# A delta-net stage in a new fixed order: values after the inversion, weights one item ahead, raw loads in GpSimd's queue

## The chip, the cores and the metric

The kernel runs on one core of a Trainium2 chip. The metric is the device time of one execution in microseconds, taken as the median of several runs. A profiled execution gives a trace of the same program; times "at" something are microseconds from the start of its span.

## The reference

Two layers, each a mixer and a convolutional feed-forward block, both with a residual and a layer norm. Layer 0's mixer is the gated delta net, to which the whole change belongs; layer 1's is a retention. Everything is fp32, sequence 1024, width 1024. The delta net, cut to what matters:

```python
proj = h @ w_in                                   # q, k, v: 8 heads x 128 each; z; a, b
qkv = silu(causal_dwconv(qkv, conv_w))            # 4 taps
q, k = l2norm(q) * dk**-0.5, l2norm(k);  beta = sigmoid(b)
gc = cumsum(-exp(a_log) * softplus(a + dt_bias))  # in each chunk
kk = where(strict, (k * beta) @ k.T * decay, 0)   # decay = exp(gc_i - gc_j), causal
u, w = solve(kk + eye, [v * beta, k * beta * exp(gc)])
qk = where(causal, q @ k.T * decay, 0)
def step(state, ...):                             # over chunks
    v_new = u - w @ state
    o = (q * exp(g)) @ state + qk @ v_new
    state = state * exp(g_last) + (k * exp(g_last - g)).T @ v_new
o = rmsnorm(o) * norm_w * silu(z)
return o @ w_out
```

The kernel takes chunks of 128 instead of the reference's 64, which is the same sum in another grouping.

## The kernel before

**Stages.** A matrix product is done as three float32r products (`mm3`): each operand is split into a high and a low part (`split`: ScalarE copies the high part, VectorE subtracts it). Up to some 78 us the kernel computes the conditioning vector, the modulated input `hT` in two halves of 512 positions, and the first projections. From there to about 620 us runs the delta net proper. Then comes `gate_phase` (output times the silu of z) and `layer_tail` (output projection, norm, feed-forward), and layer 1.

**The delta net's order.** It is written as Python generators, one for each stream of work, and `run` (L725) merges them: it keeps a clock `clk` of TensorE time, in which every matmul has a cost, and always resumes the runnable stream with the lowest priority number. A stream yields a number (wake me so many us later on that clock; these are the latencies in `LAT`), a tuple from `after_ev` (wake me once these events are emitted) or a condition (`take`: wait for buffers of a kind). Each matmul of that part goes through `pq` (L705), which chains it to the one before: TensorE's order is therefore fixed when the program is built, whatever then happens on the chip. The other engines' orders are set by the framework's own scheduler.

The streams that matter here, for heads in pairs p = 0..3 and quads g = 0, 1:

- `t_decay(p)` (L831): the decay matrices U of the pair's heads, in `aux` tiles (four exist; the recurrence of a head gives one back). It waits for the gates, for the pair before it (event `DD`, p - 1) and, in the second quad, for the first quad's inversion.
- `t_path(g)` (L843): for each head of the quad two groups of eight key products k kT, `LAT["kk"]` = 3.6 us apart, normalized into U (L872); then the inversion of 32x32 blocks by a loop of small VectorE operations (L889 to L894), two transposes and a ScalarE copy (L898 to L902). Event `T`.
- `t_chain(p)` (L913): copies the inverted blocks into tiles R and T0 on ScalarE, VectorE and GpSimd (L928, L930, L950), emits `T0`, waits `LAT["T0"]` = 8 us and then assembles the 128x128 inverses by small matmuls (32x32, then 64x64).
- `prep(p)` (L1006): transposes the pair's value features on TensorE into `acc` banks, and VectorE multiplies them out of there (L1014); then the same for decayed keys.
- `scan(p, h)` (L1050): the recurrence over eight chunks. `tail(p, h, q4)` (L1104): per half, the norm of the output (its power on GpSimd, L1111), transpose, and the store of `oTd` to DRAM from ScalarE's queue (L1118).
- `filler(items)` (L1150): all remaining projections, with the lowest priority: TensorE does them when no other stream can run. An item `("c", t)` is a projection with convolution, `"s"` the same with the result parked in DRAM (`qd`), a later `"c"` of a parked key loads it back, `"z"` is a gate projection (stored as `zd`), `"h"` finishes one begun before. Each has 48 matmuls of 128x128 by 128x512. Its weights are fetched by `load_w` (L100) when the item begins. After each item `bg_step` runs a unit of background work, among it loads of `ada_w` tiles (`mvw`, L227), which share the two buffers of the weights' tag `wr`.

PSUM has eight banks in this kernel: four `acc`, two `mm`, two `sc`.

**The gate phase** (L1224): for each head a tile `zg` of the stored gates is loaded, the output is loaded back as `raw` (two loads of 256 KB, L1242), and VectorE multiplies the two (L1243). Both loads are issued in SP's queue, which issues in order. Each raw load also sets `anchor["x", 0]`: the loads of x rows and of an `ada_b` row for the output projection are put behind the last of them in SP's queue (`after(key)`, L214 and L292).

Of the kernel before, what the change touches and what calls it, by code (L numbers as in the profile page):

```python
# [16 lines left out]
D = 1024  # L17
# [4 lines left out]
GH = 8  # L22
# [11 lines left out]
def trunk_kernel(ctx: ExitStack, tc, A):  # L34
    nc = tc.nc
    pe, act, dve, pool, sp = nc.tensor, nc.scalar, nc.vector, nc.gpsimd, nc.sync
# [45 lines left out]
    def hs(half):  # L82
        return slice(half * HALF, (half + 1) * HALF)

    xs = [dr.tile([S, D], F32, tag=f"xs{i}", name=f"xs{i}") for i in range(3)]
    oTd = [dr.tile([GH, P, S], F32, tag="oTd0", name="oTd0")]
# [5 lines left out]
    anchor = {}  # L92
# [4 lines left out]
    def kn(ap):  # L97
        return ap.rearrange("p (k n) -> p k n", n=P)

    def load_w(src, tags=("wh", "wl"), raw="wr", eng=dve):  # L100
        wr = tl(raw, [P, D])
        anchor["w"] = sp.dma_start(wr, src)
        wh = tl(tags[0], [P, D], F32R, name="wh")
        wl = tl(tags[1], [P, D], F32R, name="wl")
        split(wh, wl, wr, eng)
        return kn(wh), kn(wl)
# [73 lines left out]
    for k in range(KT):  # L180
        w = tl("hTa", [P, D], name="mvw")
# [313 lines left out]
    ssq = {}  # L495
# [223 lines left out]
    def after_ev(*names):  # L719
        return ("ev", names)  # L720
# [108 lines left out]
            give(home, 2)  # L829

    def t_decay(p):  # L831
        yield after_ev(("g",), ("DD", p - 1), ("T", p // 2 - 1))
        for h in pairs[p]:
            yield from take("aux", 1)
            U[h] = tl("aux", [P, NCH, P], name="U")
            yield from decay(h)
        yield LAT["mm"]
        for h in pairs[p]:
            act.activation(flat(U[h]), flat(U[h]), AF.Exp)
            sp.dma_start(Ld[h], flat(U[h]))  # L840
        emit(("DD", p), LAT["exp"])

# [162 lines left out]

    def prep(p):  # L1006
        heads = pairs[p]
        yield after_ev(("T", p // 2), *[("f", 2 * GH + h) for h in heads])
        for q4 in range(2):
            for h in heads:  # L1010
                pt = acc_tile()
                for c in range(4):
                    ptr(pt[:, c * P:(c + 1) * P], fx(2 * GH + h, q4 * 4 + c))
                dve.tensor_tensor(v4(feats[2 * GH + h][q4]), v4(pt), bc(ir[h][:, q4s(q4)], P), ALU.mult)  # L1014
                yield LAT["mm"]
        emit(("v", p))
        yield after_ev(("Ufree", p))
        for h in heads:
            for q4 in range(2):
                pt = acc_tile()  # L1020
                for c in range(4):
                    ptr(pt[:, c * P:(c + 1) * P], fx(GH + h, q4 * 4 + c))
                dve.tensor_tensor(U[h][:, q4s(q4)], v4(pt), bc(edl[:, q4s(q4), h], P), ALU.mult)
                yield LAT["mm"]
        emit(("kd", p))
# [122 lines left out]
            emit(("f", h), LAT["ld"])  # L1148

    def filler(items):  # L1150
        for kind, ti in items:
            if kind == "c" and ti in away:
                yield from take("qkv", 2)
                feats[ti] = two("qkv", F32, "qkv")
# [4 lines left out]
            if kind == "h":  # L1159
# [9 lines left out]
                else:  # L1169
                    emit(("f", first[ti]), LAT["fv"])  # L1170
                continue
            w = load_w(A["gdn_wz" if kind == "z" else "gdn_wqkv"][ti])
            prev = None
            if kind != "z":
                feats[ti] = []
# [20 lines left out]
            if kind != "z":  # L1196
# [5 lines left out]
                    emit(("f", ti), LAT["fv"])  # L1202
            bg_step(acc_tile)

    LAT = {"kk": 3.6, "exp": 3.2, "ld": 6.0, "g1": 12.0, "gm": 3.0, "mm": 2.2, "T": 6.0, "X": 3.4, "fs": 4.85, "T0": 8.0, "t1": 2.0, "t2": 3.3, "t3": 1.7, "D": 2.7, "s1": 1.9, "s2": 1.4, "s3": 1.8, "tail": 12.5, "ssq": 9.3, "fv": 4.0}
    events["T", -1] = events["DD", -1] = 0.0
    pairs = [(2 * p, 2 * p + 1) for p in range(GH // 2)]
    c, z = "c", "z"
    K, V = GH, 2 * GH
    s = "s"  # L1210
    quads = [tuple(range(4)), tuple(range(4, 8))]
    items = [("h", 1), ("h", 2), ("h", 3), (c, K + 2), (c, K + 3), (z, 0), (c, V), (c, V + 1), (c, V + 2), (c, V + 3), (c, 1),
             (s, 2), (s, 3), (s, K + 4), (s, K + 5), (z, 1), (z, 2), (z, 3), (c, K + 4), (c, K + 5), (c, K + 6),
             (c, K + 7), (s, 6), (s, 7), (c, V + 4), (c, V + 5), (c, V + 6), (c, V + 7), (c, 4), (c, 5),
             (z, 4), (z, 5), (z, 6), (z, 7)]
    todo = [(-1.0, gates()), (9.0, filler(items)), (0.3, t_path(0)), (2.3, t_path(1)), (0.9, load_q(1)), (2.9, load_q(3))]
    for p in range(4):
# [6 lines left out]
    def gate_phase(units, mixer, n, tags, early=(), held={}):  # L1224
        raws = []
        for k in range(n):
            gs = []
            if k in early:
                g = tl("aux", [P, S], name="zg")
                sp.dma_start(g, zd[k])  # L1230
                gs = [g[:, hs(hf)] for hf in range(2)]
                bg_step()
            else:
                accs = gemm_feat(units[k], hT)
                for hf in range(2):
                    cv = tl("cv", [P, 516], name="sg")[:, 0:HALF]
                    act.activation(cv, accs[hf], AF.Silu)
                    gs.append(cv)
            raw = held.get(k) or two(tags[k], F32, "raw")
            for hf in range(2):  # L1240
                if k not in held:
                    anchor["x", mixer] = sp.dma_start(raw[hf], oTd[mixer][k][:, hs(hf)])  # L1242
                dve.tensor_tensor(raw[hf], raw[hf], gs[hf], ALU.mult)  # L1243
            raws.append(raw)
        return raws
# [507 lines left out]
    g1 = two("auh", F32, "g1")  # L1753
# [81 lines left out]
    for t in range(4):  # L1835
        x = tl("cv", [P, 516], name="xlo")[:, 0:HALF]
# [271 lines left out]
```

## Time and profile before

| | us |
|---|---|
| median of 3 runs | 2917.15 |
| the runs | 2920.1, 2917.15, 2911.29 |
| profiled execution | 2919.49 |
| its span | 2917.7 |
| delta net, gate phase and start of the output projection | 78 to 660 |

| DMA issues touched by the change | count, KB each | us to landing (median) |
|---|---|---|
| `wr<-in_gdn_wqkv`, SP | 24, 512 | 3.5 |
| `wr<-in_gdn_wz`, SP | 8, 512 | 3.6 |
| `mvw<-in_ada_w`, SP (whole kernel) | 80, 512 | 4.5 |
| `raw<-oTd`, SP | 16, 256 | 3.5 |
| `zg<-zd`, SP | 8, 512 | 5.4 |

How to read the rows further down: PE is TensorE's matmuls, PEld its weight loads, DVE VectorE, ACT ScalarE, POOL GpSimd, SP the engine that issues most DMAs; "SPq" and "POOLq" are DMA issues in these engines' queues. A row gives engine, line, operation, `out<-in`, shapes and how many were merged. Matmuls are pipelined, so the length of one (0.4 us) is more than its pitch; the pitch is read from long rows of them.

### The profile page before, as it was taken

To read this page: it belongs to the slowest core of one execution; us is meant where nothing else is said; L and a number is where in the kernel's file an instruction comes from. 1 tells how busy PE (TensorE), PEld (TensorE's weight loads), DVE (VectorE), ACT (ScalarE), POOL (GpSimd) and SP (SyncE) were. 2 spreads that over 40 slices of the span, in tenths; PEclk is the share of its full clock that TensorE was granted. 3 is DMA by queue.
4 is the path that set the end of the run, shared out by engine and by line. 5 is a ranking of instruction groups with operands and counts; after the bars stand their busy time and mean duration, and the time that the engine had idled before them with its cause. 6 is when DMAs were issued, how large, how long until landed. Compare 5 with 4: busy or idle time off the path is not lost.

```text
span 2917.7 us, 38768 instructions
## 1 busy us (share of the span) xinstructions
PE 2799.6 (96%) x13594; PEld 2288.3 (78%) x13594; DVE 2183.0 (75%) x3874; ACT 1299.3 (45%) x2387; POOL 494.8 (17%) x509
## 2 busy tenths in 40 slices
PE   8999999999999999998999999999999999999997
PEld 6787887877788788887877877777777788888886
DVE  6796678576789888768677665666688877777779
ACT  4754564444654444545333332222344644444543
POOL 0301311000023232200000022422202023331001
PEclk9998999999999999999999999999999999999999
DMA  7223332274355555855343374755664163434853
GB/s 282 94 79 100 123 127 81 80 255 150 104 170 170 191 182 168 292 163 169 130 148 115 117 241 150 215 169 173 196 220 144 55 201 134 143 128 162 289 181 116
DMA packets 252884, 467.40 MB, mean 160 GB/s; under 512 B 24144, under 2 KB 77776, under 8 KB 252688
## 3 DMA queue, kind: packets, MB, share of 16 engines
q1 hardware_dynamic: 217984, 409.07, 42.5%
q10 hardware_dynamic: 32064, 47.20, 4.4%
q0 software_dynamic: 2640, 8.65, 0.8%
q8 instruction: 107, 1.75, 0.3%
q14 instruction: 89, 0.73, 0.1%
HBM read 347.91 MB, written 116.92 MB: 159 GB/s over the span
## 4 chain that ended last, share of the span: by engine, by line
PE 68%; DVE 16%; DMA 8%; ACT 4%; issue 3%; POOL 1%; SPq 0%; ACTq 0%; DVEq 0%; POOLq 0%
PE acc L714 14%; PE acc L1272 8%; PE acc L110 5%; PE acc L111 5%; PE acc L112 5%; PE sc L1272 4%; PE acc L1570 4%; PE sc L714 4%; PE mm L714 3%; PE sc L110 2%; DVE o L1704 2%; PE sc L111 2%; PE sc L112 2%; DMA mvw<-in_ada_w 2%; DVE wb L90 2%
## 5 line engine op out<-in xcount | busy, mean ns | idle before, releaser
L714 PE MATMUL acc<-hT,wh 128*128 128x512 f32 x960 | 301.8, 396 | 0.0
L1570 PE MATMUL acc<-bb,ab 128*128 128x512 f32 x984 | 237.0, 399 | 14.1 <-DVE bb L90 12.4
L1570 PEld LDWEIGHTS acc<-bb,ab 128*128 128x128 f32 x984 | 186.8, 192 | 58.4 <-DVE bb L90 16.7
L714 PEld LDWEIGHTS acc<-hT,wh 128*128 128x128 f32 x960 | 184.1, 192 | 35.2
L1272 PE MATMUL acc<-T,wb 128*128 128x512 f32 x840 | 203.6, 391 | 8.3 <-DVE wb L90 8.1
L89 ACT ACTIVATE ab<-ar 128x512 fp32r<-128x512 f32 x210 | 130.2, 626 | 174.0 <-PE mm L303 46.5
L714 PE MATMUL acc<-hT,wl 128*128 128x512 f32 x480 | 200.6, 418 | 3.1 <-DVE wl L90 2.0
L90 DVE TENSOR_TENSOR ab<-ar,ab 128x512 fp32r<-128x512 f32 x210 | 147.6, 708 | 64.9 <-ACT ab L89 64.8
L411 POOL TENSOR_TENSOR xg<-xg,gb 128x512 f32<-128x512 f32 x48 | 63.6, 1327 | 772.2 <-DMA xg<-xs 468.7
L1272 PEld LDWEIGHTS acc<-T,wb 128*128 128x128 f32 x840 | 156.6, 188 | 46.2 <-DVE wb L90 11.1
L90 DVE TENSOR_TENSOR wl<-wr,wh 128x1024 fp32r<-128x1024 f32 x98 | 123.4, 1259 | 81.7 <-ACT wh L89 81.3
L89 ACT ACTIVATE wh<-wr 128x1024 fp32r<-128x1024 f32 x98 | 103.7, 1059 | 158.8 <-PE acc L714 60.0
L1735 POOL TENSOR_TENSOR o<-o 128x512 f32<-128x512 f32 x80 | 125.5, 1578 | 285.2 <-PE acc L112 185.2
L90 DVE TENSOR_TENSOR wb<-wr,wb 128x512 fp32r<-128x512 f32 x162 | 115.6, 718 | 71.9 <-ACT wb L89 71.7
L90 DVE TENSOR_TENSOR wb<-mm,wb 128x512 fp32r<-128x512 f32 x216 | 145.8, 684 | 25.3 <-ACT wb L89 24.5
L1704 DVE SCALAR_TENSOR_TENSOR o<-g,vc,o 128x512 f32<-128x512 f32 (+2 forms) x176 | 156.9, 909 | 4.4 <-ACT o L1699 3.8
L89 ACT ACTIVATE wb<-mm 128x512 fp32r<-128x512 f32 x216 | 124.3, 596 | 75.3 <-DVE mm L1326 71.3
L1342 ACT ACTIVATE pc<-acc 128x512 f32<-128x512 f32 x143 | 84.7, 592 | 139.4 <-PE acc L1272 91.4
L89 ACT ACTIVATE wb<-wr 128x512 fp32r<-128x512 f32 x162 | 98.6, 627 | 106.7 <-DMA wr<-in_ffn_up 45.8
L714 PE MATMUL acc<-wh,hT 128*128 128x512 f32 x384 | 135.0, 415 | 1.0 <-DVE vv L90 1.0
L110 PE MATMUL acc<-T,wb 128*128 128x512 f32 x292 | 115.3, 395 | 5.4 <-DVE wb L90 5.4
L239 DVE SCALAR_TENSOR_TENSOR ada<-mvw,e,ada 128x512 f32<-128x512 f32 x140 | 105.4, 753 | 18.2 <-DMA mvw<-in_ada_w 17.9
(671 smaller groups left out, 7375.5 us busy)
## 6 DMA issues: line engine op xcount, KB each, us to landing
wr<-in_ffn_up SPq DMA_DIRECT2D x92, 512.0 KB, 4.2
mvw<-in_ada_w SPq DMA_DIRECT2D x80, 512.0 KB, 4.5
ad<-o SPq DMA_DIRECT2D x154, 256.0 KB, 3.1
ar<-ad SPq DMA_DIRECT2D x154, 256.0 KB, 3.7
Br<-in_ffn_down SPq DMA_DIRECT2D x88, 256.0 KB, 3.4
wr<-in_ret_wv SPq DMA_DIRECT2D x32, 512.0 KB, 4.2
ar<-od SPq DMA_DIRECT2D x56, 256.0 KB, 5.3
wr<-in_gdn_wqkv SPq DMA_DIRECT2D x24, 512.0 KB, 3.5
```

The costliest lines, as they stand in the source:

```text
L89: act.activation(dst_h, src, AF.Copy)
L90: eng.tensor_tensor(dst_l, src, dst_h, ALU.subtract)
L110: mm(acc, wl[:, k], hl[0], start=first, stop=False)
L111: mm(acc, wh[:, k], hl[1], start=False, stop=False)
L112: mm(acc, wh[:, k], hl[0], start=False, stop=last)
L239: dve.scalar_tensor_tensor(a, wr[:, kk], e[:, k:k + 1], a, ALU.mult, ALU.add)
L714: pq(pe.matmul(out, lhsT, rhs, start=start, stop=stop), cost)
L1272: return pe.matmul(*a, skip_group_check=True, **kw)
L1342: act.activation(t, X, AF.Copy)
L1570: return pe.matmul(*args, skip_group_check=True, **kw)
L1704: dve.scalar_tensor_tensor(tv, gv[:, c0 - j:c1 - j], w[:, 2 - j:3 - j], tv, ALU.mult, ALU.add)
L1735: (dve if fp == 0 else pool).tensor_tensor(o[d], o[x], o[y], op)
```

## The change

It has six parts.

1. `t_decay` of pairs 2 and 3 no longer waits for the pair before.
2. `prep` waits for the event `T0` of both pairs of its quad, where it waited for `T`, and then for a new latency `v` of 6 us.
3. The distance `kk` between two groups of key products is 4.4 instead of 3.6.
4. `filler` holds one fetched weight ahead: `fetch(i)` looks for the next item from i on that needs weights (not one of kind `h`, not the reload of a parked key) and calls `load_w` for it; an item takes its weights from there, and at once fetches those of the next.
5. The list of items is in another order: the parked queries 2 and 3 and query 1 stand ahead of values 0 to 3, and gate item 3 behind keys 6 and 7. The set of items is the same.
6. In `gate_phase` the raw loads are issued by GpSimd (`pool.dma_start`). The anchor is no longer set, so the x rows and the `ada_b` row have none.

```diff
     def t_decay(p):
-        yield after_ev(("g",), ("DD", p - 1), ("T", p // 2 - 1))
+        yield after_ev(("g",), ("DD", -1 if p > 1 else p - 1), ("T", p // 2 - 1))
...
     def prep(p):
         heads = pairs[p]
-        yield after_ev(("T", p // 2), *[("f", 2 * GH + h) for h in heads])
+        yield after_ev(("T0", p & 2), ("T0", p | 1), *[("f", 2 * GH + h) for h in heads])
+        yield LAT["v"]
...
     def filler(items):
-        for kind, ti in items:
+        wnext = []
+
+        def fetch(i):
+            parked = set()
+            for j, (kind, ti) in enumerate(items):
+                if kind == "s":
+                    parked.add(ti)
+                elif kind == "h" or (kind == "c" and ti in parked):
+                    continue
+                if j >= i:
+                    wnext.append(load_w(A["gdn_wz" if kind == "z" else "gdn_wqkv"][ti]))
+                    return
+
+        for i, (kind, ti) in enumerate(items):
...
-            w = load_w(A["gdn_wz" if kind == "z" else "gdn_wqkv"][ti])
+            if not wnext:
+                fetch(i)
+            w = wnext.pop()
+            fetch(i + 1)
...
-    LAT = {"kk": 3.6, "exp": 3.2, "ld": 6.0, "g1": 12.0, "gm": 3.0, "mm": 2.2, "T": 6.0, "X": 3.4, "fs": 4.85, "T0": 8.0, "t1": 2.0, "t2": 3.3, "t3": 1.7, "D": 2.7, "s1": 1.9, "s2": 1.4, "s3": 1.8, "tail": 12.5, "ssq": 9.3, "fv": 4.0}
+    LAT = {"kk": 4.4, "v": 6.0, "exp": 3.2, "ld": 6.0, "g1": 12.0, "gm": 3.0, "mm": 2.2, "T": 6.0, "X": 3.4, "fs": 4.85, "T0": 8.0, "t1": 2.0, "t2": 3.3, "t3": 1.7, "D": 2.7, "s1": 1.9, "s2": 1.4, "s3": 1.8, "tail": 12.5, "ssq": 9.3, "fv": 4.0}
...
-    items = [("h", 1), ("h", 2), ("h", 3), (c, K + 2), (c, K + 3), (z, 0), (c, V), (c, V + 1), (c, V + 2), (c, V + 3), (c, 1),
-             (s, 2), (s, 3), (s, K + 4), (s, K + 5), (z, 1), (z, 2), (z, 3), (c, K + 4), (c, K + 5), (c, K + 6),
-             (c, K + 7), (s, 6), (s, 7), (c, V + 4), (c, V + 5), (c, V + 6), (c, V + 7), (c, 4), (c, 5),
+    items = [("h", 1), ("h", 2), ("h", 3), (c, K + 2), (c, K + 3), (z, 0), (s, 2), (c, 1), (s, 3), (c, V), (c, V + 1), (c, V + 2), (c, V + 3),
+             (s, K + 4), (s, K + 5), (z, 1), (z, 2), (c, K + 4), (c, K + 5), (c, K + 6),
+             (c, K + 7), (z, 3), (s, 6), (s, 7), (c, V + 4), (c, V + 5), (c, V + 6), (c, V + 7), (c, 4), (c, 5),
              (z, 4), (z, 5), (z, 6), (z, 7)]
...
     def gate_phase(units, mixer, n, tags, early=(), held={}):
                 if k not in held:
-                    anchor["x", mixer] = sp.dma_start(raw[hf], oTd[mixer][k][:, hs(hf)])
+                    pool.dma_start(raw[hf], oTd[mixer][k][:, hs(hf)])
```

## The prediction

> **What bounds the kernel now.** I read the page's busy shares and chain first, then busy time by stretch, then TensorE's timeline with the idle time ahead of each group.
>
> ```profile
> PE 2799.6 (96%) x13594; PEld 2288.3 (78%) x13594; DVE 2183.0 (75%) x3874; ACT 1299.3 (45%) x2387; POOL 494.8 (17%) x509
> PE 68%; DVE 16%; DMA 8%; ACT 4%; issue 3%; POOL 1%; SPq 0%; ACTq 0%; DVEq 0%; POOLq 0%
> ...
> 78.00:660.00 582.00, 553.99 (x3675) 473.47 (x3674) 430.80 (x1047) 301.63 (x654) 100.62 (x153) 0.97 0.36 119
> 225.00:245.00 20.00, 14.48 (x71) 11.85 (x70) 18.41 (x35) 17.05 (x39) 8.50 (x22) 0.91 0.42 130
> 480.00:500.00 20.00, 14.45 (x131) 12.26 (x130) 16.44 (x29) 12.61 (x35) 8.91 (x20) 0.83 0.25 80
> 620.00:650.00 30.00, 25.80 (x111) 19.96 (x110) 20.82 (x30) 7.12 (x9) 0.00 (x0) 1.00 0.90 321
> ```
>
> The last five rows are stretches: start and end, length, busy time of PE, PEld, DVE, ACT and POOL, granted clock, DMA share, GB/s. The change touches only the stretch from 78 to 660 us. TensorE is busy 554.0 of its 582 us, so nothing there can be won beyond 28 us of idle time and what the lowered clock costs. More than a third of the idle time lies in two stretches of 20 us (5.5 us each), the only quoted ones with a clock well below 1. There the two triangular inversions end (heads 0 to 3, then 4 to 7). The waits, one row each (start, length, engine, line; in brackets the idle time ahead and who ended it):
>
> ```profile
> 131.43 1.16 PE L714 MATMUL mm<-qkv 128*128 128x128 f32 x8 [1.54 <-DVE U L872]
> 175.17 0.50 PE L714 MATMUL acc<-hT,wl 128*128 128x512 f32 x1 [1.58 <-DVE wl L90]
> 236.72 1.12 PE L717 MATMUL acc<-cst,qkv 128*128 128x128 f32 x4 [4.41 <-ACT sq L509]
> 241.82 0.50 PE L714 MATMUL acc<-hT,wl 128*128 128x512 f32 x1 [1.11 <-ACT sq L509]
> 412.89 1.16 PE L714 MATMUL mm<-qkv 128*128 128x128 f32 x8 [1.35 <-DVE U L872]
> 456.25 0.50 PE L714 MATMUL acc<-hT,wl 128*128 128x512 f32 x1 [0.46 <-DVE wl L90]
> 489.95 1.11 PE L717 MATMUL acc<-cst,qkv 128*128 128x128 f32 x4 [5.55 <-DVE qkv L1014]
> ```
>
> At 236.72 and 489.95 TensorE stands in front of value transposes, for want of a free acc bank (four exist): the earlier ones have not been emptied, because ScalarE and VectorE are copying the blocks of the finished inversion:
>
> ```profile
> 231.97 3.42 ACT L930 ACTIVATE R<-RX 32x128 f32<-32x128 f32 x8 [0.33 <-DVE RX L898]
> 237.29 3.96 ACT L930 ACTIVATE T<-TX 32x256 f32<-32x256 f32 x6
> 484.90 3.88 ACT L930 ACTIVATE T<-TX 32x256 f32<-32x256 f32 x6
> 485.10 2.83 DVE L928 COPY T<-TX 32x256 f32<-32x256 f32 x6
> 487.96 1.34 DVE L90 TENSOR_TENSOR wl<-wr,wh 128x1024 fp32r<-128x1024 f32 x1
> 489.22 1.27 DVE L1014 TENSOR_TENSOR qkv<-acc,ir 128x512 f32<-128x512 f32 x2
> ```
>
> The value products (L1014) come only at 489.22, behind copies and a weight split. TensorE's order is pinned, so the projections behind the transposes could not pass them.
>
> **The change, part by part.**
>
> *Values later.* The value transposes now wait until both pairs have issued their block copies, and then 6 us. TensorE gets projections for that time instead; the first solve product stands at 8 us as before. No work is removed. At the second inversion the transposes then fall near 481 + 6 = 487 and the solve near 489, and the copies end at 484.90 + 3.88 = 488.8: little waiting is left. At the first they fall near 237 and 239, while ScalarE's copies end at 237.29 + 3.96 = 241.25. The squares that stand between its two copy groups belong to a query projection which the new list places some 40 us earlier, and that pulls the end towards 239. Projections fill acc banks too, and ScalarE must empty them beside the copies, so I leave 3 us of the 4.41 + 1.11 + 5.55 = 11.1. Gain 8, with bounds of 11.1 and -4 (rival C).
>
> *The clock behind the gaps.* In the chain of waits (start, length, what):
>
> ```profile
> 175.17 27.53 PE acc L714 x120
> ...
> 491.07 3.84 PE acc L714 x9
> ```
>
> A projection matmul takes 27.53/120 = 0.229 us, even behind the 1.58 us wait, and 3.84/9 = 0.427 behind the 5.55 us one. Those nine lost 1.8 us. The first inversion has a lesser lag (clock 0.91 against 0.83); I take 1.2 there. Gain 3, bounds 0 and 5.
>
> *Weights one item ahead.* No new instruction: each load and split is issued an item earlier. Only the waits on wl at 175.17 and 456.25 go: 2.0 us. All other splits were already hidden by the item before. A load ahead holds one of the two wr buffers for longer, which the ada_w tiles share; by the alternation of the two that costs nothing as long as VectorE consumes an ada_w tile within an item of 48 x 0.229 = 11 us. Gain 2; the other bound is a loss of 3.2, a wait like that at 175.17 once more in each inversion.
>
> *Key products 4.4 instead of 3.6 us apart.* This lets TensorE do 0.8 us more of other work between two groups, of which there are 16. Both waits on U L872 go: 2.9 us. But the inversions begin later, by 16 x 0.8 = 12.8 us at most. The projections that are left hide this:
>
> ```profile
> 365.40 0.60 ACT L1194 ACTIVATE sg<-acc 128x512 f32<-128x512 f32 x1
> ...
> 375.92 0.89 PE mm L714 x8
> ...
> 609.54 0.39 PE L714 MATMUL mm<-w,DT 128*128 128x128 f32 x2
> ...
> 611.76 5.49 PE acc L714 x24
> ```
>
> After the last product of the recurrence (609.54) there are still the 24 projection matmuls of the last row and two groups of 6, 36 x 0.229 = 8.2 us. So up to 8.2 us of a longer chain cost nothing, and 4.6 of the 12.8 show. The new list gives some back: the fourth gate item, whose second half is emptied at 365.40, moves behind the key projections, and head 4's key, which waited for it (375.92, the first key group of the second inversion), is reloaded up to 11 us sooner. Against that, the decay of heads 6 and 7 no longer waits for that of 4 and 5: the second of the aux tiles which come free goes to head 6, and head 5 waits for the other pair's recurrence. I can't see that as a gain; I let the two cancel by half and put down a loss of 2 (bounds 0 and 7).
>
> *Raw loads in GpSimd's queue.* 16 loads of 256 KB leave SP's queue, where each held up what stood behind it until its head's store had landed (SP's timeline, and the loads by line with their median us to landing):
>
> ```profile
> 617.27 0.80 SPq L1242 DMA_DIRECT2D raw<-oTd  x2
> ...
> 624.06 0.81 SPq L1242 DMA_DIRECT2D raw<-oTd  x2
> ...
> 626.52 0.69 SPq L102 DMA_DIRECT2D wr<-in_gdn_wout  x1
> ...
> 634.02 0.50 PE L327 MATMUL acc<-wl,hl 128*128 128x512 f32 x1 [1.72 <-DVE wl L90]
> 646.09 0.73 PE L326 MATMUL acc<-wh,hl 128*128 128x512 f32 x2 [1.78 <-ACT wh L89]
> 648.62 0.50 PE L327 MATMUL acc<-wl,hl 128*128 128x512 f32 x1 [0.70 <-DVE wl L90]
> ...
> raw<-oTd SPq DMA_DIRECT2D x16, 256.0 KB, 3.5
> ...
> xg<-xg POOLq DMA_DIRECT2D x32, 256.0 KB, 2.4
> ...
> 845.45 0.76 POOL L413 DMA_DIRECT2D xg<-xg  x1 [0.31 <-POOL xg L412]
> ```
>
> The out-projection's last weight (626.52) stood behind two raw loads at 624.06, and its split ends the wait of 1.72 at 634.02. That wait goes. The x rows lose their anchor behind the last raw load and may start sooner, which spreads the full DMA load of 620 to 650 (share 0.90) and may take the waits of 1.78 and 0.70 too. GpSimd pays 16 x 0.76 us, in a stretch where it has 0.00 us of work. What queues behind a waiting raw load there are the recurrence's norms:
>
> ```profile
> L1111 POOL TENSOR_TENSOR so<-so,mhalf x16: 998/1007/1389, 315.0 to 613.7; 128x4 f32<-128x4 f32 x16
> ```
>
> The last is at 613.7; if it stands behind a load which waits out a store and lands in the trace's 3.5 us, the tail of the stage is late by that much for each of the last two pairs. Gain 1.7, bounds 4.2 and -7.
>
> [...]
>
> *What a new order brings of its own.* The old one has misjudged waits that this change does not aim at:
>
> ```profile
> 127.79 0.71 PE L714 MATMUL sc<-gm,m_lowr 128*128 128x512 f32 x2 [1.48 <-DVE U L828]
> 135.22 0.73 PE L714 MATMUL sc<-gm,m_lowr 128*128 128x512 f32 x2 [1.24 <-POOL raw L482]
> 595.28 0.49 PE L714 MATMUL mm<-Sn,qkv 128*128 128x128 f32 x2 [1.39 <-DVE qkv L1092]
> ```
>
> They sum to 4.1. They stay, and I charge the same once more: a loss of 4 (bounds 0 and 10).
>
> The sum: -8 - 3 - 2 - 2.9 + 2 - 1.7 + 4 = -11.6, about 12 us. From the profiled execution's 2919.49 that is 2907.5; this execution is 2.3 above the median of the three runs, 2917.15, so the median comes to **2905**.
>
> **The rivals.**
>
> A, the forecast: the two gaps mostly close. 2905, between 2895 and 2911.
>
> B, the gaps move: TensorE arrives at the solve just as early and stands there until the copies are done, with the lower clock behind it as before. For it: the copies take 3.42 + 3.96 us on ScalarE in any order. Against it: they end within a few us of the solve's new place. Left are 2.0 + 2.9 + 1.7 less 2 + 4, nothing to speak of: 2916.
>
> C, the other side: the acc banks. During the copies the projections, two halves of 5.5 us, take the banks that the values held, and only ScalarE empties them, whose copies take 7.4 us. TensorE stands for 7.4 instead of 5.5 us at each inversion, 4 us more in all; the values, now in the solve's time, put eight products of 0.64 us (1.27/2) in front of its VectorE copies, 5.1 us at each. With 4 + 10.2, less the 4.9 for the wl and U waits, plus the 2 and the 4, it is 15 slower: 2932. It decides once no bank is free 6 us after the inversion. Against it: ScalarE is idle for part of 480 to 500 (12.6 of 20 busy), so it can empty a bank between copies.
>
> D, GpSimd's queue: raw loads stand in front of norms, 2 x 3.5 us late at the end, and the rest as in A: 2905 + 7 + 1.7 = 2914.
>
> **How the numbers follow.** This kernel's runs tell a change from none at about 0.3% (8.8 us: 2908.4 and 2925.9). A 0.55, B 0.19, C 0.16, D 0.10. Faster: 0.9 of A, and a tenth of B and D, about 0.53, and I add 0.04 because the x rows and the clock can both give more than I took: 0.57. Slower: C and little else, 0.16. The same: 0.27. The range must reach past B and D to the foot of C and down to where all the bounds of gain are met (11.1 + 5 + 2 + 2.9 + 4.2 = 25 us): **2891 to 2928**; A's own is 2895 to 2911.
>
> **What would show it.** Right: no wait over 2 us on TensorE where the inversions end, value transposes in among the solve's small matmuls, projections at 0.229 us ahead of it, TensorE idle under 18 us between 78 and 660. Wrong: a wait of 4 us or more ahead of the solve (B), or of projections on an acc bank with ScalarE as releaser (C); rows in which the norms wait for DMA (D); TensorE out of projections before the last recurrence product, so that the chain and not the projections sets the end.

## The result, and the profile after

| | us |
|---|---|
| kernel before, median of 6 runs | 2917.56 (2911.29 to 2922.9) |
| changed kernel, median of 6 runs | 2934.01 (2929.49 to 2939.46) |
| ratio, 95% interval | 1.0059 [1.0041, 1.0076] |
| profiled execution of the changed kernel, its span | 2929.49, 2927.4 |

One execution of a kernel further down (decay alone: 3996.69 us at a granted clock of 0.654) was in a slower state and is left out of its median and ratio.

The change makes the kernel 0.6% slower; the forecast was 0.4% faster. On the page of the changed kernel the work is the same: TensorE has 13594 matmuls as before, which take 6.6 us longer, and its share of the chain that ended last falls from 68% to 58%; VectorE gains 3 points of it, DMA and ScalarE 2 each.

```profile
PE 2806.2 (96%) x13594; PEld 2295.3 (78%) x13594; DVE 2182.6 (75%) x3874; ACT 1293.5 (44%) x2385; POOL 511.2 (17%) x525
...
PE 58%; DVE 19%; DMA 10%; ACT 6%; issue 4%; POOL 2%; SPq 1%; DVEq 0%; ACTq 0%; POOLq 0%
```

The stretch from 78 to 660 us, of the changed kernel (length, busy time of PE, PEld, DVE, ACT and POOL, granted clock, DMA share, GB/s):

```profile
78.00:660.00 582.00, 548.22 (x3622) 472.36 (x3623) 420.39 (x1035) 291.20 (x647) 114.36 (x169) 0.95 0.35 117
```

TensorE's idle time there has grown from 28.0 to 33.8 us (the prediction named under 18 as the sign of being right) and the clock has fallen from 0.97 to 0.95. To see where, the stage is cut into six stretches, first of the kernel before:

```profile
75.00:225.00 150.00, 143.03 (x679) 117.33 (x678) 123.22 (x309) 92.72 (x183) 32.29 (x44) 1.00 0.29 93
225.00:300.00 75.00, 68.39 (x723) 60.45 (x722) 48.82 (x101) 30.15 (x67) 8.68 (x23) 0.86 0.30 95
300.00:475.00 175.00, 172.14 (x944) 147.08 (x943) 138.02 (x376) 101.14 (x219) 41.83 (x57) 1.00 0.37 122
475.00:545.00 70.00, 63.11 (x718) 55.97 (x717) 45.54 (x95) 30.02 (x84) 9.39 (x21) 0.90 0.15 50
545.00:600.00 55.00, 53.61 (x367) 48.34 (x366) 34.68 (x101) 26.14 (x69) 5.42 (x5) 1.00 0.45 150
600.00:720.00 120.00, 112.31 (x516) 90.82 (x515) 81.27 (x138) 49.72 (x70) 5.17 (x7) 0.99 0.59 206
```

and then of the changed kernel:

```profile
75.00:225.00 150.00, 147.15 (x706) 121.77 (x704) 123.42 (x304) 97.70 (x204) 33.67 (x47) 1.00 0.31 99
225.00:300.00 75.00, 67.17 (x710) 60.16 (x709) 51.24 (x106) 25.07 (x50) 10.92 (x23) 0.84 0.30 96
300.00:475.00 175.00, 168.16 (x926) 144.56 (x925) 129.66 (x359) 96.47 (x215) 42.67 (x55) 0.99 0.34 113
475.00:545.00 70.00, 62.90 (x660) 55.03 (x659) 46.69 (x103) 29.99 (x81) 10.60 (x23) 0.85 0.20 65
545.00:600.00 55.00, 55.00 (x398) 50.89 (x397) 30.71 (x86) 22.12 (x64) 8.78 (x13) 1.00 0.27 94
600.00:720.00 120.00, 107.32 (x500) 86.84 (x499) 86.56 (x158) 51.02 (x81) 10.55 (x16) 0.94 0.63 222
```

Two losses can be read from each row: idle time (length less PE busy) and what the lowered clock costs, put here, as an estimate, at (1 - clock) x PE busy (a projection matmul of the kernel before takes 0.229 us in the rows from 175.17, at a clock of 1.00, and 0.427 in those from 491.07, at 0.50), good to a us or so a row because the clock has two places. The kernel before loses 32.4 + 17.0 us, the changed one 37.3 + 28.3: 16.2 more, of which 4.9 idle and 11.3 clock. By stretch, both together: -4.1, +2.4, +5.7, +3.3, -1.4, +10.3. So the waits ahead of the first inversion went, as was meant; the two inversion ends (second and fourth stretch) lost 5.7 instead of giving back 11; and the end of the stage lost most. The last matmul of the output projection (L328) starts at 723.9 before and 736.8 after, 12.9 later. The bookkeeping is 3.3 us above that, about as much as its rounding allows over six rows.

TensorE's timeline of the changed kernel, the rows where it waited (start, length, engine, line, operation; in brackets the idle time ahead and who ended it):

```profile
239.87 1.04 PE L717 MATMUL acc<-cst,qkv 128*128 128x128 f32 x8
247.10 1.06 PE L714 MATMUL mm<-T,U 32*32 32x32 f32 x16 [6.19 <-ACT T L930]
...
367.07 0.66 PE L717 MATMUL acc<-cst,qkv 128*128 128x128 f32 x4 [2.94 <-DVE U L828]
...
495.32 0.50 PE L714 MATMUL acc<-hT,wl 128*128 128x512 f32 x1 [2.61 <-ACT sq L509]
...
504.98 2.08 PE L714 MATMUL acc<-qkv 128*128 128x128 f32 x8 [2.57 <-ACT qkv L488]
...
621.24 0.62 PE L714 MATMUL acc<-hT,wh 128*128 128x512 f32 x2
621.70 0.38 PE L714 MATMUL mm<-w,DT 128*128 128x128 f32 x2
...
627.37 0.99 PE L717 MATMUL acc<-cst,qkv 128*128 128x128 f32 x4 [2.53 <-DVE qkv L1113]
629.99 1.08 PE L717 MATMUL acc<-cst,qkv 128*128 128x128 f32 x4 [1.62 <-DVE qkv L1113]
...
648.12 0.80 PE L327 MATMUL acc<-wl,hl 128*128 128x512 f32 x1 [3.31 <-DVE wl L90]
```

Four things are to be seen. At 247.10 the gap of the first inversion stands in front of the solve (6.19 us), where rival B put it. At the second inversion no such gap stands in front of the solve, but there are two waits of 2.61 and 2.57 us that ScalarE ends, the first of them of a projection for an acc bank (rival C's releaser, though below the 4 us that it named). At 621.70 the last product of the recurrence comes behind the last projection (621.24), the last of the prediction's signs of being wrong; in the kernel before, 36 projection matmuls were still to come at that point, and TensorE had work until the normalized outputs came. Now TensorE waits for them, at 627.37 and 629.99. And the splits of the output projection's weights are late at 648.12. ScalarE and VectorE show why the solve waits:

```profile
239.96 1.99 ACT L900 ACTIVATE TP<-T 128x1024 f32<-128x1024 f32 x1
246.40 3.90 ACT L930 ACTIVATE T<-TX 32x256 f32<-32x256 f32 x6 [1.15 <-DVE TX L902]
```

```profile
238.96 1.25 DVE L898 STREAM_TRANSPOSE RX<-T 128x1024 f32<-128x1024 f32 x1
240.18 0.75 DVE L490 SCALAR_TENSOR_TENSOR oq<-raw,vc,oq 128x512 f32<-128x512 f32 x1
240.84 3.49 DVE L928 COPY R<-RX 32x128 f32<-32x128 f32 x8
244.36 0.84 DVE L490 SCALAR_TENSOR_TENSOR oq<-raw,vc,oq 128x512 f32<-128x512 f32 x1
245.13 1.23 DVE L902 STREAM_TRANSPOSE TX<-TP 128x1024 f32<-128x1024 f32 x1
```

The loop of the inversion ends where the first transpose (L898) begins. In the kernel before that row is

```profile
230.69 1.24 DVE L898 STREAM_TRANSPOSE RX<-T 128x1024 f32<-128x1024 f32 x1
```

so the first inversion ends 8.3 us later than before, while the solve begins at the same time (247.00 before, 247.10 now). The second transpose (L902) comes 6.2 us after the first: ScalarE's copy for it (L900) ends only at 241.95, and then VectorE has block copies and the convolutions of the query that the new list puts there. The copies from it end at 250.3, 11.3 us after the start of the first transpose (10.6 before). The order allows 8 us of TensorE's time from event `T` to the solve, and TensorE's last work ahead of the solve ends at 240.91. So by the order `T` falls near 233, some 6 us before the first transpose begins; in the kernel before the two went together (the value transposes, which waited for `T`, stand at 230.84).

### The profile page after: what moved, and what is told of

Read it like the earlier page. It is cut to its first block, busy times and chain, and to the rows that moved or that the text cites. A ratio compares the mean times of both kernels' runs of the same rounds, so it can differ in the third digit from the quotient of the medians.

```text
span 2927.4 us, 38787 instructions
## 1 busy us (share of the span) xinstructions
PE 2806.2 (96%) x13594; PEld 2295.3 (78%) x13594; DVE 2182.6 (75%) x3874; ACT 1293.5 (44%) x2385; POOL 511.2 (17%) x525
## 4 chain that ended last, share of the span: by engine, by line
PE 58%; DVE 19%; DMA 10%; ACT 6%; issue 4%; POOL 2%; SPq 1%; DVEq 0%; ACTq 0%; POOLq 0%
PE acc L714 8%; PE acc L1289 6%; PE acc L1587 4%; PE acc L110 4%; PE acc L111 4%; PE acc L112 4%; PE sc L714 4%; PE sc L1289 3%; DMA mvw<-in_ada_w 3%; PE mm L714 3%; DVE o L1721 2%; DVE wb L90 2%; DMA wr<-in_ffn_up 2%; DVE qkv L490 2%; PE sc L110 1%
```

## The experiments

All times are medians beside runs of the kernel before on the same chip; "+" is us slower than that. The last column is where the last addition of the recurrence (L1092, the product of the `mm` bank) starts in the one profiled execution. It is good to some 6 us only: the two profiles of the changed kernel have 623.3 and 629.4, and both executions took 2929.4 to 2929.5 us.

| kernel | median | against before | ratio, 95% interval | last addition |
|---|---|---|---|---|
| kernel before | 2917.56 | | | 610.0 |
| changed kernel | 2934.01 | +16.5 | 1.0059 [1.0041, 1.0076] | 623.3 |
| changed kernel, once more (after_again) | 2930.27 | +13.3 | 1.0045 [1.003, 1.0059] | 629.4 |
| changed without kk (no_kk) | 2925.53 | +6.0 | 1.0023 [1.001, 1.0035] | 612.4 |
| without values (no_values) | 2927.58 | +8.1 | 1.0027 [1.0013, 1.0041] | 618.8 |
| without raw loads (no_pool) | 2928.0 | +8.5 | 1.003 [1.0018, 1.0041] | 629.9 |
| without decay (no_decay) | 2921.91 | +4.9 | 1.0011 [0.9998, 1.0025] | 620.8 |
| without the list (no_items) | 2924.46 | +7.5 | 1.0023 [1.0011, 1.0034] | 619.6 |
| without fetch (no_fetch) | 2921.69 | +4.7 | 1.0014 [0.9999, 1.0029] | 616.6 |
| before with kk alone (only_kk) | 2917.88 | -1.7 | 0.9995 [0.9983, 1.0007] | 609.2 |
| decay alone (only_decay) | 2918.83 | +1.7 | 1.0004 [0.9991, 1.0017] | 599.5 |
| fetch alone (only_fetch) | 2919.91 | +2.8 | 1.0008 [0.9996, 1.0021] | 609.8 |
| raw loads alone (only_pool) | 2912.52 | -4.1 | 0.9992 [0.9977, 1.0007] | 611.4 |
| values alone (only_values) | 2927.52 | +10.9 | 1.004 [1.0026, 1.0054] | 613.8 |
| values, second quad alone (values_2) | 2923.62 | +6.1 | 1.0015 [1.0, 1.0029] | 613.2 |
| kk and raw loads (kk_pool) | 2919.91 | +2.3 | 1.0013 [0.9997, 1.0028] | 606.4 |
| second inversion late (late6) | 2913.74 | -2.9 | 0.9994 [0.9984, 1.0003] | 600.2 |
| second inversion later (late12) | 2920.9 | +4.3 | 1.0017 [1.0003, 1.0032] | 619.2 |
| changed, T0 = 14 (after_t0) | 2927.59 | +10.4 | 1.0039 [1.0023, 1.0056] | 628.2 |
| changed, wait filled (after_warm) | 2931.7 | +14.5 | 1.0047 [1.0034, 1.006] | 621.1 |

**One part undone.** Each kernel is the changed one with one part put back; the sixth is the list of items as in the diff above. after_again is the changed kernel itself.

```diff
 no_kk:      -"kk": 4.4   +"kk": 3.6
 no_decay:   -("DD", -1 if p > 1 else p - 1)   +("DD", p - 1)
 no_pool:    -pool.dma_start(raw[hf], ...)   +anchor["x", mixer] = sp.dma_start(raw[hf], ...)
 no_fetch:   -w = wnext.pop(); fetch(i + 1)   +w = load_w(...)
 no_values:  -after_ev(("T0", p & 2), ("T0", p | 1), ...); yield LAT["v"]   +after_ev(("T", p // 2), ...)
```

> The changed kernel with the key groups 3.6 us apart again. Theory 1 (the inversion chain sets the time, and the wider spacing starts both inversions later): the first inversion's start comes back from 178.6 to about 173 us, the second's from 438 to about 427, and the time falls by 9 to 14 us, to 2920 to 2925. Theory 2 (the values' new place, or GpSimd's queue, costs the time, and the projections hide a later inversion): within 3 us of the changed kernel, 2931 to 2937, with the waits on U L872 back.

> The changed kernel with the value transposes at their old place, right behind the inversion. Theory 1: the gap at the end of each inversion stays (TensorE stops at the values instead of at the solve), time within 4 us of the changed kernel, 2930 to 2938. Theory 2: the time falls by 8 us or more, below 2926.

> The changed kernel with the raw loads in SP's queue again. Theory 1: the gate phase gave or took little, 2930 to 2938. Theory 3 (raw loads wait in GpSimd's queue ahead of the norms and land later, so the out-projection starts late): the last product of raw and gate comes about 3 us sooner after the last store, the wait of 3.31 us ahead of the out-projection's second half shrinks below 2, and the time falls by 3 us or more, below 2931.

> The changed kernel once more, so that the undone parts stand beside it on one chip: ratio to the kernel before 1.004 to 1.008.

> The changed kernel in which the decays of heads 6 and 7 wait for those of 4 and 5 again. Theory 1 (the inversion chain sets the time; letting heads 6 and 7 in gives one of the two early aux tiles to head 6, so head 5's decay, and with it the first key group of the second inversion, comes late): the first key group of the second inversion comes at 378 us or sooner instead of 385.8, the second inversion starts 6 to 9 us sooner, and the time falls by 5 to 9 us against the changed kernel of the same chip. Theory 2 (that wait is hidden): within 2 us of the changed kernel.

> The changed kernel with the old list of items. Theory 1: key 4 is reloaded after gate item 3 again, but its first key group waits for the decay of head 5 anyway: the second inversion's start moves by less than 3 us and the time by less than 4 us against the changed kernel of the same chip. Theory 2 (the new list itself is wrong: values 0 to 3 come just ahead of the inversion's end and their convolutions load VectorE there): the first inversion takes 58 us from start to end instead of 60.4, and the time falls by 4 us or more.

> The changed kernel with weights loaded when the item begins. Theory 1: two waits on wl of 2 us in all come back, nothing else: 0 to 4 us slower than the changed kernel of the same chip. Theory 2 (the splits that are issued an item ahead get in front of the inversion's operations on VectorE): the first inversion is 2 us shorter or more, and the time falls by 2 to 6 us.

By the medians each undone part gives something back, 5 to 9 us measured against after_again (no_kk, no_values and no_pool ran on another chip than it). Only decay and fetch have intervals that lie clear of after_again's, and theirs just reach down to the kernel before. The six sum to 40 us (7.3 + 5.2 + 4.8 + 8.4 + 5.8 + 8.6), three times the loss of 13.3. The surplus of 27 us has an uncertainty of some 23, because after_again's own interval of 4 us to each side enters it five times. So the parts' costs do not simply add, as far as these intervals show, and of the other four none carries the whole.

In no_kk the second inversion begins at 426.25, where it begins in the kernel before (426.02); in the changed kernel it is 439.85.

**One part alone.** The same lines the other way, in the kernel before. The list alone was not run.

> The kernel before with nothing but the spacing of 4.4 us. Theory 1: 5 to 6 us later at each inversion, 8 to 13 us slower than before, 2925 to 2930. Theory 2 and the prediction's term: the two waits of 1.54 and 1.35 go and up to 4.6 us show, so between 3 us faster and 2 us slower, 2914 to 2919.

> The kernel before with the decay part alone. If the parts' costs add (undone in the changed kernel it gave 8.4 us back): 8 us slower than before, ratio 1.0029. If each delay alone is covered by projections that are left over, and only together they pass that cover: within 3 us of before, ratio 0.999 to 1.001.

> The kernel before with the weights fetched one item ahead, alone. If the parts' costs add (undone in the changed kernel it gave 8.6 us back): 8 to 9 us slower than before, ratio 1.003. If each alone is covered: within 3 us of before; the prediction of this term by itself was 2 us faster.

> The kernel before with the raw loads in GpSimd's queue, alone. The prediction's term: 1.7 us faster. If the loads land later from there and the last products of output and gate with them (16.8 us from the last store to the last of these products in the changed kernel, 9.9 in the kernel before): 3 to 6 us slower, ratio 1.001 to 1.002.

> The kernel before with the values part alone. The prediction's term: 8 us faster, and some 3 us for the clock, ratio 0.996 to 0.997. If the wait only moves to the solve, because the copies and VectorE's work there take 10 to 11 us in any order: a wait of 4 us or more in front of the first product of the solve, and within 3 us of before (0.999 to 1.001). If the values part is a loss by itself: undone in the changed kernel it gave about 5 us back, ratio 1.0018.

Four parts alone cost nothing that can be measured; the upper ends of their intervals allow 2 to 6 us each. The values part alone costs 10.9 us, most of the change's loss; by the prediction it was the largest gain. Its profile, first TensorE's waits at the two inversion ends:

```profile
240.35 2.18 PE L717 MATMUL acc<-cst,qkv 128*128 128x128 f32 x8 [3.84 <-ACT sq L509]
...
496.23 1.97 PE L717 MATMUL acc<-cst,qkv 128*128 128x128 f32 x8 [3.30 <-ACT qkv L491]
```

then its stretches,

```profile
225.00:300.00 75.00, 70.12 (x717) 61.78 (x717) 46.97 (x93) 29.02 (x65) 8.78 (x23) 0.82 0.26 89
300.00:475.00 175.00, 169.69 (x923) 145.76 (x922) 135.54 (x370) 99.85 (x217) 43.11 (x55) 0.98 0.35 118
475.00:545.00 70.00, 65.50 (x698) 57.53 (x697) 46.99 (x97) 29.63 (x79) 10.73 (x23) 0.88 0.17 58
```

then a wait in the recurrence between the inversions,

```profile
329.42 1.23 PE L714 MATMUL sc<-Sn,qkv 128*128 128x128 f32 x4 [2.06 <-DVE qkv L1093]
```

and the decayed keys, by line, with the first and the last start (us), for the first and the second quad, of the kernel before and of values alone:

```profile
L1023 DVE TENSOR_TENSOR U<-acc,eg x8: 682/688/692, 267.5 to 293.1; 128x512 f32<-128x512 f32 x8
L1023 DVE TENSOR_TENSOR U<-acc,eg x8: 680/688/692, 516.0 to 540.6; 128x512 f32<-128x512 f32 x8
```

```profile
L1024 DVE TENSOR_TENSOR U<-acc,eg x8: 678/684/692, 274.5 to 293.8; 128x512 f32<-128x512 f32 x8
L1024 DVE TENSOR_TENSOR U<-acc,eg x8: 680/687/692, 527.6 to 547.7; 128x512 f32<-128x512 f32 x8
```

Idle time at the two inversion ends fell by 1.7 and 2.4 us (6.61 and 6.89 before, 4.88 and 4.50 now). The waits did not go away: the value transposes still stand for a bank that ScalarE holds, 7.1 us together against 11.1. But the clock costs more in all three rows: 12.6 + 3.4 + 7.9 = 23.9 us against 9.6 + 0 + 6.3 = 15.9. Idle time and clock together, the two inversion ends come out 0.5 us worse than before, and the stretch between them 5.8 worse: there the recurrence of the first quad waits 2.06 us for VectorE, and the clock behind that wait is 0.50 from 330 to 335. Another 4.8 are lost from 600 to 720. The decayed keys, which `prep` issues behind the values, begin 7.0 and 11.6 us later in the two quads and end 0.7 and 7.1 later. The recurrence, which `scan` starts behind its pair's keys, begins 3.1 and 12.2 us later (ScalarE's first copy of a product, 287.6 to 290.7 and 534.8 to 547.0), but its last addition only 3.8. In the second quad a part of this comes from ahead: the inversion itself begins at 430.2 instead of 426.0.

The same part in the second quad alone:

```diff
     def prep(p):
+        if p > 1:
+            yield after_ev(("T0", p & 2), ("T0", p | 1), *[...])
+            yield LAT["v"]
+        else:
+            yield after_ev(("T", p // 2), *[...])
-        yield after_ev(("T", p // 2), *[...])
```

> The kernel before with the values part for the second quad alone (values 0 to 3 at the end of the inversion as before, values 4 to 7 after T0 and 6 us). The values part in both quads made it 10.9 us slower, with decayed keys and the recurrence behind the values in each quad. If each quad brings its own delay and these add: about half, 4 to 7 us, ratio 1.0015 to 1.0025. If only their sum passes what the left-over projections cover (a second inversion that ended 10 us later cost nothing, one that ended 12.5 us later 4): within 3 us of before. If the second quad alone is the loss, because only there few projections are left: 9 to 12 us, ratio 1.003 to 1.004.

The ratio, 1.0015, is 4.4 us: about half, as if each quad brought its share. The interval, 0 to 8.5 us, also touches the case in which it is hidden. It ends below the 9 to 12 us expected for the second quad as the whole loss, but overlaps the interval of the values part itself (7.6 to 15.8), so that case is unlikely and not excluded.

**The chain made late without any of the parts.** GpSimd is made to hold the tile that the second inversion needs, in the kernel before; no other engine gets work, and the order is told.

```diff
         emit(("X", g))
-        yield LAT["X"]
+        yield LAT["X"] + (12.0 if g == 1 else 0.0)      # late6: 6.0
...
+        if g == 1:
+            pool.tensor_copy(T, X)
+            for _ in range(12):                          # late6: 6
+                pool.memset(T, 0.0)
         pool.memset(T, 0.0)
```

> The kernel before with the second inversion made to start about 12 us later, by a copy and twelve more memsets of T on GpSimd (no load for VectorE, ScalarE or TensorE), and the order told so (X + 12 in the second quad). None of the six parts is in it. In the changed kernel that inversion starts 13.7 us later than in the kernel before, 12 of it behind the first projections. Theory 1 (a later second inversion is the loss: the projections that are left over cover the first part of it, the rest comes through to the end): 5 to 12 us slower, ratio 1.002 to 1.004, TensorE idle in 600 to 660 at least 4 us more than in the kernel before. Theory 2 (the loss is TensorE's idle time and lowered clock at the inversions, and the later second inversion is a mere companion): within 3 us of before. The prediction's cover of 8.2 us would give 4.

> The same with a copy and six memsets, about 6 us later, X + 6. Theory 1: all of it covered, within 3 us of before. If there is no cover at all and the chain sets the end from the first us: 6 us slower, ratio 1.002.

VectorE's loop of the second inversion begins, in the kernel before, late6, late12 and the changed kernel:

```profile
426.02 0.21 DVE L892 TENSOR_TENSOR fs<-Y,T 128x31 f32<-128x31 f32 x1
```

```profile
434.12 0.21 DVE L896 TENSOR_TENSOR fs<-Y,T 128x31 f32<-128x31 f32 x1 [1.98 <-POOL T L891]
```

```profile
439.54 0.21 DVE L896 TENSOR_TENSOR fs<-Y,T 128x31 f32<-128x31 f32 x1 [0.87 <-POOL T L891]
```

```profile
439.85 0.20 DVE L892 TENSOR_TENSOR fs<-Y,T 128x31 f32<-128x31 f32 x1
```

8.1 us late costs nothing, 13.5 us late costs 4.3 (0.9 to 9.3 by the interval). The changed kernel is 13.8 us late at this point, so this lateness by itself accounts for about a third of its loss. In late12 TensorE ends its projections before the recurrence and then waits for the last outputs:

```profile
618.24 0.88 PE L714 MATMUL mm<-w,DT 128*128 128x128 f32 x4
626.22 1.12 PE L717 MATMUL acc<-cst,qkv 128*128 128x128 f32 x4 [5.16 <-DVE qkv L1116]
```

That is what the end of the changed kernel looks like, made by lateness alone. In late6, however, the last addition starts at 600.2, 10 us before that of the kernel before, although the inversion is later: a new deal of the order mattered more there than 8 us of inversion. So late6 never drew on the projections at the end, and does not test how much they cover.

**TensorE's wait at the solve, filled in two ways.** after_t0 tells the order that the solve comes 14 us after the inversion; after_warm puts 24 extra matmuls into the wait, whose result is overwritten.

```diff
-"T0": 8.0
+"T0": 14.0
```

```diff
         pa = mm_tile()
+        if p == 0:
+            for i in range(24):
+                pm(pa, m_lowr, hT[0][i % 8][0], cost=0.0)
```

> The changed kernel with the latency T0 at 14 us instead of 8: the order then puts some 6 us more of projections between the end of an inversion and the first product of the solve, and as many fewer at the end of the stage. Theory 1 (the order sends TensorE to the solve before the block copies are done; the wait of 6.19 us there and the clock of 0.50 behind it are what is lost): the wait falls under 2 us, the granted clock of 245 to 275 rises from 0.60 to 0.8 or more, and the kernel is 4 to 9 us faster than the changed kernel, 2921 to 2926. Theory 2 (the chain of inversion, solve and recurrence sets the end, and TensorE's idle time in the middle is harmless): the projections moved forward are missing at the end; the idle time of 620 to 660 grows by what the wait loses and the time stays within 2 us of the changed kernel, 2928 to 2932.

> The changed kernel with 24 extra matmuls of 128x128 by 128x512 (5.5 us, their result is overwritten) in front of the first product of the first solve, inside the wait of 6.19 us; the order is otherwise the same, and no projection is moved. If the idle time lowers the clock and the lowered clock lengthens what follows: the clock of 245 to 270 rises from about 0.53 to 0.9 or more, and although work was added the kernel is 4 to 9 us faster than the changed kernel. If the lowered clock comes from the small products of the solve and not from the idle time: the clock stays at 0.5 from 250 to 265 and the time within 2 us of the changed kernel. If the clock rises and the time still stays within 2 us: the chain on VectorE sets the end, and a slow TensorE there costs nothing.

With T0 at 14 the projections did move in front of the solve, but the first of them stood behind the value transposes for a bank that VectorE had not emptied, and what was moved was missing at the end:

```profile
249.81 0.79 PE L714 MATMUL acc<-hT,wl 128*128 128x512 f32 x1 [7.37 <-DVE qkv L1015]
```

```profile
PE acc L717 <- DVE qkv L1113: 9.2, 1, 9.2
```

The first row is a wait of the timeline, the second the waits for normalized outputs between 590 and 670 (us in all, times, longest). The wait kept its length in another place, and the time stayed that of the changed kernel within the intervals: 2927.59 is 0.4 us below the band of theory 2 and above that of theory 1.

after_warm did fill the wait. Its clock behind it (same columns as the other stretches):

```profile
245.00:250.00 5.00, 4.08 (x85) 3.31 (x84) 4.73 (x10) 4.53 (x7) 3.74 (x9) 1.00 0.01 3
250.00:255.00 5.00, 5.00 (x100) 4.63 (x99) 2.06 (x3) 2.35 (x4) 0.00 (x0) 0.70 0.82 265
255.00:260.00 5.00, 5.00 (x161) 5.00 (x157) 2.30 (x8) 0.00 (x0) 0.00 (x0) 0.50 0.01 3
```

The solve now starts at full clock, and falls to 0.50 among its own small products, with TensorE idle for no more than 0.9 us after the fill (4.08 of 5 busy in the first row). Ratio 1.0047 against 1.0045 and 1.0059 for the changed kernel: no gain that these intervals show; they would hide one of some 5 us. The extra matmuls do none of the kernel's work, and the solve waits for the same copies (it begins at 246.45 instead of 247.10), so only the clock behind the wait is tested. From 225 to 300 that rose from 0.84 to 0.91, some 4 us by the bookkeeping, and the time does not show it. What the 6 us of idle time would be worth with useful work in them is not shown.

**A selection.** The two parts whose medians alone lay below the kernel before, together, with both lines as above:

> The kernel before with the key products 4.4 us apart and the raw loads in GpSimd's queue, the two parts whose medians alone were below the kernel before (1.6 and 4.1 us, neither beyond its interval). If they add: 0.998, some 6 us faster, faster than both kernels. If they meet as the six parts do: 1.000 to 1.002.

1.0013 [0.9997, 1.0028]: they do not add to a gain. No kernel tried beats the one before by more than its interval.

## Why the prediction was wrong, by its own steps

**Values later, forecast -8, measured +10.9 alone.** This step failed. It counted TensorE's idle time ahead of the transposes as the price, and took it that projections in its place would win it back. The runs show three things in its place: the wait stays (3.84 and 3.30 us for a bank that ScalarE holds, rival C's releaser, though ahead of transposes and not of projections; with all six parts 6.19 in front of the solve, which is rival B's sign); the lowered clock costs 8 us more in the three stretches, so that the inversion ends come out 0.5 us worse where 8 + 3 better were forecast; and the decayed keys begin 7.0 and 11.6 us later, the recurrence behind them 3.1 and 12.2. The prediction costed the move of the values but not of the keys that the same stream issues behind them.

**The clock, forecast -3.** The sign was wrong: with the six parts it cost 4.3 us more at the two inversion ends (15.9 before, 20.2 now) and 11.3 more in the whole stage. The step took it that less idle time means less time at low clock. Values alone has less idle time than the kernel before in the three stretches shown (14.7 against 16.4 us) and a lower clock.

**Weights ahead, forecast -2.** Both waits on wl at 175 and 456 are gone from the timeline, and alone the part gives +2.8 with an interval that holds zero: the mechanism is right, the gain isn't to be seen.

**Key products, forecast -2.9 and +2.** Both waits on U L872 are gone, and alone it comes to -1.7 with zero in the interval. Alone it moves the second inversion by 1.2 us only (427.2 against 426.0), not by up to 12.8. The cover of 8.2 us agrees with late12, where 13.5 us of lateness cost 4.3 (13.5 - 8.2 = 5.3, with an interval of 0.9 to 9.3); late6 does not test it. But the cover was charged to this part only. With all six parts none of it is left at 621.70. The decay part, said to cancel, is nothing alone; with the others TensorE stands 2.94 us at 367.07 behind those decays.

**Raw loads, forecast -1.7.** Alone -4.1, zero in the interval; nothing speaks against the term, and no gain is shown either. In the changed kernel rival D's sign shows at the end, in GpSimd's timeline:

```profile
626.93 1.14 POOL L1259 DMA_DIRECT2D raw<-oTd  x2 [0.36 <-issue]
628.09 1.03 POOL L1112 TENSOR_TENSOR so<-so,mhalf 128x4 f32<-128x4 f32 x1
```

The last norm stands behind two raw loads, 1.2 us of issuing, and the output of it is what TensorE waits 1.62 us for at 629.99: a tenth part of the loss, not the 7 us of D.

**The new order's own waits, forecast +4, bounds 0 and 10.** Mis-sized. The waits of the changed kernel that the prediction did not foresee sum to some 16 us in the rows shown alone (2.94 + 2.61 + 2.57 + 2.53 + 1.62 + 3.31), beyond the bound of 10.

**The sum.** The parts were summed as if each had the stage to itself. Alone the five tried sum to +9.6 us (-1.7 + 1.7 + 2.8 - 4.1 + 10.9), of which only the values stand out; all six give 13 to 16; and all but the values still give 8.1, though four of these five alone give nothing that can be measured. What they may share is the room between the end of the recurrence and the end of the projections. In the table all kernels whose last addition starts by 611.4 have intervals that hold 1; of the thirteen in which it starts later ten lie beyond 1 and three reach down to it. That is an ordering over kernels and no proof, and between 611.4 and 613.8 it is finer than the 6 us by which two profiles of one kernel differ. The rivals stood nearer: C's 2932 is close to the 2934, and the values in the solve's time are the part that cost most; but it priced the wait for banks as growing, and that shrank, so its number is in part luck.

What stays open: how the loss divides between the clock and the late recurrence. The bookkeeping gives 11 us of clock and 5 of idle time, but some 4 us of clock won back by filling the largest wait did not show in the time. It is not settled either why the five parts other than the values cost 8 us together. The list, which is the fifth, was not run alone, and the intervals of the other four leave room for much of the 8. The trace of no_values says where it goes: TensorE is idle 9.9 us at the second inversion end (475 to 545; 6.9 before), 9.23 of them in one wait that ScalarE ends, and 15.1 us from 600 to 720 (7.7 before), with a wait of 8.11 for the normalized outputs.

## What to carry to other kernels

TensorE's gaps in this fixed order were a symptom of what ended last there (the block copies and the banks); more of the kernel's work in front of one only moved it (6.19 us ahead of the solve in the changed kernel, 7.37 ahead of a projection in after_t0), so change what ends last. Where a stream is moved, cost everything that the same stream issues behind it. And slack at the end of a stage is one account for all edits: charge every part to it together. A chain made late on purpose measures it, if the trace shows that the lateness arrives at the end (in late12 it did, in late6 it did not).

## What the runs showed of the hardware

In the first solve the clock fell among small products. In after_warm it falls from 1.00 to 0.50 between 250 and 260, with TensorE busy 5.00 of 5 us in both rows, 100 and 161 products, most of them the solve's. The kernel before shows the same with no wait in the 8 us ahead: TensorE is busy 5.00 of 5 us from 245 to 250 (clock 1.00, its solve begins at 247.00) and from 250 to 255, where the clock falls:

```profile
250.00:255.00 5.00, 5.00 (x77) 4.61 (x74) 1.38 (x2) 2.14 (x4) 0.00 (x0) 0.53 0.14 54
```

In its second solve, which begins at 497.88, it is 1.00 among as many small products and falls only in the row behind, to 0.63:

```profile
500.00:505.00 5.00, 5.00 (x162) 4.79 (x160) 1.29 (x2) 2.99 (x5) 0.00 (x0) 1.00 0.02 3
505.00:510.00 5.00, 4.40 (x115) 4.11 (x112) 4.10 (x15) 0.00 (x0) 0.00 (x0) 0.63 0.02 5
```

Ahead of the first solve it had fallen too, there behind the wait of 4.41 us that ends at 236.72 (0.65 from 236 to 238, 0.50 from 238 to 240), and was back a few us later:

```profile
235.00:240.00 5.00, 3.28 (x10) 2.80 (x11) 4.89 (x10) 4.93 (x20) 4.50 (x11) 0.66 0.00 0
240.00:245.00 5.00, 3.89 (x23) 3.04 (x22) 4.02 (x9) 4.26 (x8) 1.33 (x5) 1.00 0.44 129
```

So a low clock stands behind a wait in the kernel before at 235 to 240, and at 250 to 260 it stands where the record shows TensorE busy throughout. As far as the record shows it (the ends of matmuls are modelled in it), the clock does not follow there the time in which matmuls are in flight. What sets it is not shown by these runs.

The 16 raw loads, issued by GpSimd in the changed kernel, took 4.5 us from issue to landing by the median, against 3.5 from SP in the kernel before; the two kernels differ in the other five parts as well:

```profile
raw<-oTd POOLq DMA_DIRECT2D x16, 256.0 KB, 4.5
```
